# Interleaved rotary embedding, 8 rows: the last output row leaves in one cast DMA of GpSimd's queue, without an fp32 tail on SP's queue

## The chip, the cores and the metric

The kernel runs on one core of one Trainium2 chip. The metric is the device time of one execution in microseconds (us). Before the change it is 316.17 us, the median of three runs (316.14 to 316.25).

## The reference

Input x is float32 with shape (8, 2048, 16, 64): batch, sequence, heads, head dimension. The head dimension holds pairs (x1, x2) side by side, and cos and sin are float32 (2048, 32), one value per sequence position and pair.

```
x1 = x_pairs[..., 0]
x2 = x_pairs[..., 1]
out1 = x1 * cos - x2 * sin
out2 = x1 * sin + x2 * cos
out = stack([out1, out2], axis=-1)      # pairs side by side again, float32
```

It reads 67.1 MB of x and writes 67.1 MB of output.

## The kernel before

**Tiling.** A batch entry is called a row here. The 2048 positions of a row lie on 128 partitions with K = 16 positions each, so a row is a tile of 128 partitions by 16 x 1024 elements. In DRAM it is 8.39 MB of float32, and each partition's part is one contiguous piece of 65,536 bytes. In the on-chip memory it is bf16 and half that size. The pool `buf` (tile name `xt`) has five places for rows; the list `at` says which row uses which place, so that rows 5, 6 and 7 reuse the places of rows 0, 1 and 2 (at = 4, 0, 1, 2, 3, 4, 0, 1).

**Transfers.** `load` (line 57) and `store` (line 60) are DMAs issued by GpSimd (POOL in the profile). They change the type on the way: float32 in DRAM to bf16 on the chip, and back. All of them go through one queue, which the profile calls q0 (software_dynamic). Two transfers go through SP's queue, q1 (hardware_dynamic), which carries them without a change of type: the head (line 94), which is the first four of the sixteen positions of row 0, as fp32 into the tile `st`; and the tail (line 133), which is the last four positions of row 7, as fp32 out of `st`.

**Arithmetic.** VectorE (DVE) does all of it, in bf16. For one row `rotate` issues three instructions: qt = x * s_tab (line 79), x = x * c_tab (line 85), x = x + qt with each pair swapped (line 90). `qt` and `st` share one buffer (tag "work").

**Order.** It is written out by hand (`tc.manual_schedule()`). Loads and stores stand in GpSimd's program in the order of the calls, and GpSimd waits at each one until its data are ready or its place is free. The end of that program, which the change touches, is: store of rows 4 and 5, store of row 6, store of the first 12 positions of row 7. Beside the last of them come three instructions on other engines. VectorE copies a single element from row 7 into row 6's place (line 131); since that place is being read by the store of row 6, VectorE waits there until the store has landed. Then it casts the last four positions of row 7 to fp32 (line 132), and SP sends them (line 133).

**The close.** After the last instruction the framework adds a closing sequence, recorded under line 159. SP waits for the last transfer of each semaphore that DMAs use, two semaphores to a wait, and for VectorE. GpSimd runs a drain of its own. Then the engines meet, GpSimd clears the semaphores, and they meet again.

Of the kernel before, what the change touches and what calls it, by code (L numbers as in the profile page):

```python
# [2 lines left out]

# [4 lines left out]


@with_exitstack  # L10
def kernel(
    ctx: ExitStack,
    tc: tile.TileContext,
    x: bass.AP,
    cos: bass.AP,
    sin: bass.AP,
    out: bass.AP,
):
    nc = tc.nc
    fp32 = mybir.dt.float32  # L20
    bf16 = mybir.dt.bfloat16
    mult = mybir.AluOpType.mult
    add = mybir.AluOpType.add

    B, S, H, D = x.shape
    P = 128
    K = S // P
    D2 = D // 2
    HD = H * D
    NX = 5  # L30
    HEAD = 4
    TAIL = 4
    GATE = 14

    x_t = x.rearrange("b (p k) h d -> p b k (h d)", p=P, k=K)
    out_t = out.rearrange("b (p k) h d -> p b k (h d)", p=P, k=K)
    cos_t = cos.rearrange("(p k) c -> p (k c)", p=P, k=K)
    sin_t = sin.rearrange("(p k) c -> p (k c)", p=P, k=K)

    consts = ctx.enter_context(tc.tile_pool(name="consts", bufs=1))  # L40
    rows_pool = ctx.enter_context(tc.tile_pool(name="rows", bufs=1))
    stage = ctx.enter_context(tc.tile_pool(name="stage", bufs=1))

    cos_sb = consts.tile([P, K * D2], fp32)
    sin_sb = consts.tile([P, K * D2], fp32)
    c_tab = consts.tile([P, K, D], bf16)
    s_tab = consts.tile([P, K, D], bf16)


    buf = rows_pool.tile([P, NX, K, HD], bf16, name="xt")  # L50
    at = [4, 0, 1, 2, 3, 4, 0, 1]

    def place(b, n=1, k0=0, k1=K):
        return buf[:, at[b] : at[b] + n, k0:k1]

    def load(b, n=1, k0=0, k1=K):
        nc.gpsimd.dma_start(out=place(b, n, k0, k1), in_=x_t[:, b : b + n, k0:k1])  # L57

    def store(b, n=1, k0=0, k1=K):
        nc.gpsimd.dma_start(out=out_t[:, b : b + n, k0:k1], in_=place(b, n, k0, k1))  # L60

    def rotate(b, k0=0, k1=K, gate=None):
        nk = k1 - k0
        xp = buf[:, at[b], k0:k1]
        qt = stage.tile([P, K, HD], bf16, name="qt", tag="work")

        def rows(a):
            return a.rearrange("p k (h e) -> p k h e", h=H, e=D)

        def tab(a, j0=0, j1=nk):  # L70
            return dataclasses.replace(
                a,
                offset=a.offset + (k0 + j0) * D,
                ap=[a.ap[0], [D, j1 - j0], [0, H], [1, D]],
            )


        for a, z in ((0, nk),) if gate is None else ((0, GATE), (GATE, nk)):
            nc.vector.tensor_tensor(  # L79
                out=rows(qt[:, a:z]), in0=rows(xp[:, a:z]), in1=tab(s_tab, a, z), op=mult  # L80
            )
            if z < nk:
                one = buf[:1, at[gate], 0, :1]
                nc.vector.tensor_copy(out=one, in_=one)  # L84
        nc.vector.tensor_tensor(out=rows(xp), in0=rows(xp), in1=tab(c_tab), op=mult)  # L85
        q_swap = dataclasses.replace(
            qt, offset=qt.offset + 1, ap=[qt.ap[0], [2, nk * HD // 2], [-1, 2]]
        )
        x3 = xp.rearrange("p k (a j) -> p (k a) j", j=2)
        nc.vector.tensor_tensor(out=x3, in0=x3, in1=q_swap, op=add)  # L90

    with tc.manual_schedule():
        head = stage.tile([P, TAIL, HD], fp32, name="st", tag="work")
        nc.sync.dma_start(out=head[:, :HEAD], in_=x_t[:, 0, :HEAD])
        load(0, k0=HEAD)
        nc.gpsimd.dma_start(out=cos_sb, in_=cos_t)  # L96
        nc.gpsimd.dma_start(out=sin_sb, in_=sin_t)  # L97
        load(1)
        load(2)

        nc.vector.tensor_copy(out=buf[:, at[0], :HEAD], in_=head[:, :HEAD])  # L101
        s2 = s_tab.rearrange("p k (i j) -> p (k i) j", j=2)
        nc.vector.tensor_copy(out=s2[:, :, 0], in_=sin_sb)  # L103
        nc.vector.tensor_scalar_mul(s2[:, :, 1], sin_sb, -1.0)  # L104
        nc.vector.tensor_copy(  # L105
            out=c_tab.rearrange("p k (i j) -> p (k i) j", j=2),
            in_=cos_sb.to_broadcast([P, K * D2, 2]),
        )

        rotate(0, 0, HEAD)  # L110
        rotate(0, HEAD, K)
        rotate(1, gate=0)
        store(0)
        load(3, 2)
        load(5)
        rotate(2)
        store(1, 2)
        rotate(3)
        store(3)
        load(6, 2)  # L120
        rotate(4)
        rotate(5)
        store(4, 2)
        rotate(6)
        store(6)
        rotate(7)
        store(7, k1=K - TAIL)


        tail = stage.tile([P, TAIL, HD], fp32, name="st", tag="work")  # L130
        nc.vector.tensor_copy(out=buf[:1, at[6], 0, :1], in_=buf[:1, at[7], K - 1, :1])  # L131
        nc.vector.tensor_copy(out=tail, in_=buf[:, at[7], K - TAIL :])  # L132
        nc.sync.dma_start(out=out_t[:, 7, K - TAIL :], in_=tail)


# [1 line left out]
_INS = ['x', 'cos', 'sin']  # L137
_OUTS = [((8, 2048, 16, 64), 'float32')]


# [23 lines left out]
```

## Time and profile before

| | |
|---|---|
| median of three runs | 316.17 us |
| the profiled execution | 316.19 us |
| span of its trace (first to last instruction) | 314.4 us |
| time outside the span | 1.8 us |
| DVE busy | 215.1 us (68%) |
| POOL busy | 8.7 us (3%) |
| HBM read, written | 67.63 MB, 67.11 MB |
| DMA packets | 2688 |

The profile is of one execution. Its page gives the busy time of each engine, the span in 40 slices with a digit of busy tenths for each engine and for the 16 DMA engines, the DMA queues, the chain of work that ended last, and the costliest groups of instructions. Bytes are counted at the destination, so a load that writes bf16 counts for half of what it reads. "SPq" and "POOLq" are the instruction sequencers of SP and GpSimd; time in which they wait is not counted as busy. Times that are given to a thousandth are those of single records of this trace, counted from the start of the span.

### The profile page before, as it was taken

What the parts mean: (1) busy time and instruction counts of PE and PEld (TensorE: products, weight loads), DVE (VectorE), ACT (ScalarE), POOL (GpSimd) and SP (SyncE); (2) the same over time, 40 slices, a digit from 0 to 9 for tenths busy, and PEclk for the clock granted to TensorE, in tenths of its full rate; (3) what the DMA queues carried; (4) which work ended last, traced back from release to release, by engine and by line L of the source; (5) the groups of instructions that cost most, each with busy time, mean ns of one, the idle gap of its engine ahead of it and who ended that gap; (6) DMA issues with size and microseconds to landing.
All of it is one profiled execution on the core that took longest, in us unless ns stands there. A gap on an engine that the chain in (4) does not pass through costs nothing.

```text
span 314.4 us, 110 instructions
## 1 busy us (share of the span) xinstructions
DVE 215.1 (68%) x35; POOL 8.7 (3%) x18
## 2 busy tenths in 40 slices
DVE  0029999999999206999999999300009999997200
POOL 3000000100000000000000000000000000000000
DMA  8999999999999999999999999999999999999997
GB/s 261 256 283 200 200 208 258 267 400 425 308 200 200 217 250 200 200 325 475 400 400 500 434 400 400 250 217 200 200 308 425 400 400 525 409 400 400 434 440 327
DMA packets 2688, 102.24 MB, mean 325 GB/s; under 512 B 256, under 2 KB 256, under 8 KB 384
## 3 DMA queue, kind: packets, MB, share of 16 engines
q0 software_dynamic: 2400, 98.04, 96.8%
q1 hardware_dynamic: 288, 4.19, 3.3%
HBM read 67.63 MB, written 67.11 MB: 429 GB/s over the span
## 4 chain that ended last, share of the span: by engine, by line
DVE 59%; another core or an unknown queue 17%; DMA 17%; issue 0%; POOL 0%; DVEq 0%; PEldq 0%
DVE xt L85 19%; DVE xt L90 19%; DVE qt L79 19%; DMA out_dram<-xt 10%; DMA sin_sb<-in_sin_dram 7%; DVE st L132 1%; POOL xt L57 0%; DVE c_tab L105 0%; POOL cos_sb L96 0%; DVE s_tab L103 0%; DVE s_tab L104 0%; DVE xt L131 0%; DVE xt L84 0%; DVEq L79 0%
## 5 line engine op out<-in xcount | busy, mean ns | idle before, releaser
L79 DVE TENSOR_TENSOR qt<-xt,s_tab 128x16384 bf16<-128x16384 bf16 (+4 forms) x10 | 69.8, 6983 | 53.7 <-DMA xt<-in_x_dram 53.5
L90 DVE TENSOR_TENSOR xt<-xt,qt 128x16384 bf16<-128x16384 bf16 (+2 forms) x9 | 69.7, 7744 | 0.3
L85 DVE TENSOR_TENSOR xt<-xt,c_tab 128x16384 bf16<-128x16384 bf16 (+2 forms) x9 | 69.7, 7744 | 0.3
L101 DVE CAST xt<-st 128x4096 bf16<-128x4096 f32 x1 | 2.3, 2294 | 15.3 <-DMA st<-in_x_dram 15.3
L60 POOL DMA_DIRECT2D out_dram<-xt x6 | 3.6, 607 | 227.6 <-DVE xt L90 171.8
L57 POOL DMA_DIRECT2D xt<-in_x_dram x6 | 3.8, 637 | 53.0 <-DMA out_dram<-xt 52.2
L103 DVE CAST s_tab<-sin_sb 128x512 bf16<-128x512 f32 x1 | 0.5, 454 | 6.3 <-DMA sin_sb<-in_sin_dram 6.3
L131 DVE COPY xt<-xt 1x1 bf16<-1x1 bf16 x1 | 0.1, 145 | 5.7 <-DMA out_dram<-xt 5.7
L132 DVE CAST st<-xt 128x4096 f32<-128x4096 bf16 x1 | 2.3, 2272 | 0.0
L105 DVE CAST c_tab<-cos_sb 128x1024 bf16<-128x1024 f32 x1 | 0.7, 682 | 0.0
L97 POOL DMA_DIRECT2D sin_sb<-in_sin_dram x1 | 0.6, 564 | 0.0
L96 POOL DMA_DIRECT2D cos_sb<-in_cos_dram x1 | 0.6, 557 | 0.0
L104 DVE TENSOR_SCALAR s_tab<-sin_sb 128x512 bf16<-128x512 f32 x1 | 0.4, 442 | 0.0
L84 DVE COPY xt<-xt 1x1 bf16<-1x1 bf16 x1 | 0.1, 136 | 0.0
L148 POOL MEMSET const-float32-0.0<- 128x1 f32 x1 | 0.1, 99 | 0.2 <-issue 0.2
L148 POOL MEMSET const-bfloat16-1.0<- 128x1 bf16 x1 | 0.1, 102 | 0.0
L148 POOL MEMSET const-uint8-127<- 128x1 uint8 x1 | 0.1, 100 | 0.0
L148 POOL MEMSET const-float32-1.0<- 128x1 f32 x1 | 0.1, 99 | 0.0
## 6 DMA issues: line engine op xcount, KB each, us to landing
xt<-in_x_dram POOLq DMA_DIRECT2D x2, 8192.0 KB, 58.8
xt<-in_x_dram POOLq DMA_DIRECT2D x3, 4096.0 KB, 57.6
out_dram<-xt POOLq DMA_DIRECT2D x1, 6144.0 KB, 22.2
xt<-in_x_dram POOLq DMA_DIRECT2D x1, 3072.0 KB, 21.3
st<-in_x_dram SPq DMA_DIRECT2D x1, 2048.0 KB, 14.5
out_dram<-st SPq DMA_DIRECT2D x1, 2048.0 KB, 16.9
cos_sb<-in_cos_dram POOLq DMA_DIRECT2D x1, 256.0 KB, 21.3
sin_sb<-in_sin_dram POOLq DMA_DIRECT2D x1, 256.0 KB, 21.4
```

What stands on the lines that cost most here:

```text
L57: nc.gpsimd.dma_start(out=place(b, n, k0, k1), in_=x_t[:, b : b + n, k0:k1])
L60: nc.gpsimd.dma_start(out=out_t[:, b : b + n, k0:k1], in_=place(b, n, k0, k1))
L79: nc.vector.tensor_tensor(out=rows(qt[:, a:z]), in0=rows(xp[:, a:z]), in1=tab(s_tab, a, z), op=mult)
L85: nc.vector.tensor_tensor(out=rows(xp), in0=rows(xp), in1=tab(c_tab), op=mult)
L90: nc.vector.tensor_tensor(out=x3, in0=x3, in1=q_swap, op=add)
L96: nc.gpsimd.dma_start(out=cos_sb, in_=cos_t)
L97: nc.gpsimd.dma_start(out=sin_sb, in_=sin_t)
L101: nc.vector.tensor_copy(out=buf[:, at[0], :HEAD], in_=head[:, :HEAD])
L103: nc.vector.tensor_copy(out=s2[:, :, 0], in_=sin_sb)
L104: nc.vector.tensor_scalar_mul(s2[:, :, 1], sin_sb, -1.0)
L105: nc.vector.tensor_copy(out=c_tab.rearrange("p k (i j) -> p (k i) j", j=2), in_=cos_sb.to_broadcast([P, K * D2, 2]),)
L132: nc.vector.tensor_copy(out=tail, in_=buf[:, at[7], K - TAIL :])
```

## The change

The last row goes out in one call, `store(7)`, of all 16 positions through GpSimd's queue. The tail tile, the one-element copy that waits for the store of row 6, the cast to fp32 and the transfer on SP's queue are removed. The head tile takes its size from HEAD instead of TAIL; both are 4, so nothing changes there. Line numbers behind line 31 are smaller by one, and those behind the removed block by seven.

```
-    TAIL = 4
...
-        head = stage.tile([P, TAIL, HD], fp32, name="st", tag="work")
+        head = stage.tile([P, HEAD, HD], fp32, name="st", tag="work")
...
         rotate(7)
-        store(7, k1=K - TAIL)
-
-
-        tail = stage.tile([P, TAIL, HD], fp32, name="st", tag="work")
-        nc.vector.tensor_copy(out=buf[:1, at[6], 0, :1], in_=buf[:1, at[7], K - 1, :1])
-        nc.vector.tensor_copy(out=tail, in_=buf[:, at[7], K - TAIL :])
-        nc.sync.dma_start(out=out_t[:, 7, K - TAIL :], in_=tail)
+        store(7)
```

In the built programs VectorE has two instructions fewer (the copy and the cast), SP one fewer (the transfer), and GpSimd's last store has 128x16384 elements instead of 128x12288. Everything ahead of it stands in the same order with the same waits. SP's five closing waits come in another pairing, since the semaphore of its second transfer is gone. Before they are, in order: {store 7, store 6}, then three pairs of older transfers, then {tail, an older load}. After they are: {store 6}, {store 7, an older one}, then three pairs of older transfers.

## Prediction

> **What bounds the kernel.** I read the page first (engines, slices, queues), then the windows of the end, the timeline of the end, the waits of SP's queue, and the records of the closing line. From the page:
>
> ```profile
> DVE 215.1 (68%) x35; POOL 8.7 (3%) x18
> ...
> DMA  8999999999999999999999999999999999999997
> ...
> q0 software_dynamic: 2400, 98.04, 96.8%
> q1 hardware_dynamic: 288, 4.19, 3.3%
> ```
>
> No compute engine is above 68%, while the DMA digit is 9 from the second slice to the last but one, and the two queues together fill 96.8 + 3.3 = 100% of the 16 DMA engines' time. The transfers are the bound from start to end. The chain of waits names mostly DVE, but it also has 17% of "another core or an unknown queue", and DVE's own waits end on a load; DVE follows the transfers.
>
> The end of the kernel, from the timeline (start, duration, what; in brackets the idle time before it):
>
> ```profile
> 262.75 0.55 POOL L60 DMA_DIRECT2D out_dram<-xt  x1 [62.80 <-DVE xt L90]
> ...
> 279.94 8.69 DVE L90 TENSOR_TENSOR xt<-xt,qt 128x16384 bf16<-128x16384 bf16 x1
> 288.92 0.55 POOL L60 DMA_DIRECT2D out_dram<-xt  x1 [25.63 <-DVE xt L90]
> 294.28 0.14 DVE L131 COPY xt<-xt 1x1 bf16<-1x1 bf16 x1 [5.65 <-DMA out_dram<-xt]
> 294.35 2.27 DVE L132 CAST st<-xt 128x4096 f32<-128x4096 bf16 x1
> 296.65 0.35 SPq L133 DMA_DIRECT2D out_dram<-st  x1
> ```
>
> Row 7 is computed at 288.63, and its store is issued at 288.92. The store of row 6, issued at 262.75, lands only at 294.19, where L131 is released. So store 7 stands in its queue for some 4 us before the first of its packets runs. The windows show how full the DMA engines are in the two last rows (columns: stretch, length, DVE and POOL busy, clock, DMA share, GB/s):
>
> ```profile
> 274.01:293.32 19.31, 14.59 (x2) 0.55 (x1) 1.00 1.02 434
> 293.32:312.69 19.37, 2.34 (x2) 0.00 (x0) 1.00 1.02 433
> ```
>
> The first stretch is the packets of store 6, all on q0: 8.39 MB at 434 GB/s. The second is row 7, three quarters on q0 and one quarter on q1: the same bytes at 433 GB/s. There is no hole that the change could fill, and the split over two queues brings no rate.
>
> **Part 1: the transfer of row 7.** Before, a DMA engine serves 8 packets of 49,152 bytes on q0 and 32 of 16,384 bytes on q1. After, it serves 8 of 65,536 bytes on q0, as for row 6. In the packet records the 65,536-byte packets of store 6 follow each other every 2.412 us on an engine, and from the completion record of one row to that of the next (stores 5 and 6) it is 293.803 - 274.487 = 19.316 us on the engine that ends last. The mixed stretch takes 2.430 us for 49,152 + 16,384 bytes, and the 16,384-byte packets alone, with which it ends, one every 0.607 us (2.428 us for 65,536 bytes). So the last completion record moves from 313.233 to 293.803 + 19.316 = 313.119: **-0.11 us**. Bounds: 0 (both rates equal) and -0.15 (8 x 0.018). Nothing else delays store 7: its one wait is DVE L90 of row 7, as before, and its packets queue behind those of row 6, as before (between stores 5 and 6 the engine goes on 0.042 us after the completion record).
>
> A rule of the Trainium skill speaks against the change (DMA: Bandwidth & Descriptors, Specifications): a transfer of GpSimd's queue has its first byte after about 1 us, one of SP's after about 0.6 us. By it alone the last bytes would come some 0.4 us later, an estimate from that page. In this trace that start is covered: the store is issued over 4 us before its first packet at 293.336 can run.
>
> **Part 2: what is removed on DVE and SP.** L131 (0.14), L132 (2.27) and the issue of L133 (0.35) lie beside the packets of q0, which run from 293.336 to 310.799 without a hole. Nothing else waits for them but L133 itself. Their removal is worth nothing; DVE is done at 288.63, over 24 us ahead of the end. The extra 4,096 elements a partition cost GpSimd's issue nothing: the whole-row store took 0.55 us too (262.75).
>
> **Part 3: the close.** This is where the change shifts something. SP's waits and the closing records:
>
> ```profile
> SPq L159 <- DMA out_dram<-xt: 14.1, 1, 14.1
> SPq L159 <- DMA out_dram<-st: 2.2, 1, 2.2
> ```
>
> ```profile
> L159 SPq EVENT_SEMAPHORE  x7: 17/28/28, 311.2 to 314.4; - x7
> ...
> L159 POOLq DRAIN  x3: 45/96/22855, 288.9 to 314.1; - x3
> ```
>
> Before, q0 is done first. Its last completion record is at 310.799, and SP passes the wait for it at 311.156 (0.357 later). SP then passes three older waits (0.074 + 0.061 + 0.060 = 0.195 us) while the tail still runs, waits 2.2 us more, and passes the tail's wait at 313.580. GpSimd's first drain is the long one in the second fence: it starts at 288.902 and takes 22.855 us, so it ends at 311.757, which is 0.958 us after q0's last completion record. The tail on q1 covers that end: the engines meet only at 313.736, 0.156 us after SP's last wait, two short drains of SP lying between (0.065 and 0.058, then 0.033).
>
> After, q0 is the last, and both covers are gone.
> - SP: 313.119 + 0.357 = 313.476 for the wait of store 7, then the three older waits in the open (0.195), then 0.156: 313.827, **+0.09 us** against 313.736.
> - GpSimd's drain: 313.119 + 0.958 = 314.077, and 0.03 to its next instruction (the distance after its second drain): 314.106, **+0.37 us**.
>
> The later one counts. No other record shows what the long drain waits for. Bounds: if its end follows nothing of q0, it is out of the way and SP's +0.09 is left; if its delay grows with the size of the store behind it, 0.958 x 65,536 / 49,152 = 1.277 us and the sum is +0.69. I take the delay of the one row there is, 0.958.
>
> **Sum.** The profiled execution took 316.19 us (0.02 above the median). 316.19 + 0.37 = **316.56 us**; the -0.11 of the transfer is inside the 0.37. About 0.2% (0.63 us) is what a measurement of this kernel can tell from no change, so I forecast no change that counts, on the slow side of zero.
>
> **The rivals.**
> 1. *SP's chain ends last* (GpSimd's drain ends for a reason of its own): 316.19 + 0.09 = 316.28. For it: the drain's record has no wait for a semaphore, and POOL spans are rough. Against it: the drain ended within 1 us of q0's last packet after standing for 22.9 us. 19 in 100.
> 2. *Slower: GpSimd's drain trails longer.* The place is the close, where the tail gave it 313.736 - 311.757 = 2.0 us of cover; without cover it decides over 0.2% once its delay after the last completion record exceeds 0.958 + 0.26 = 1.22 us. By bytes it would be 1.277 us: 316.19 + 0.69 = 316.88. For it: a single row, and bigger packets. Against it: the same number of packets on q0 (128 and 16 completion records). 14 in 100.
> 3. *Slower: q0 starts afresh for row 7* instead of going on. On the empty queue at the start, from the issue at 1.24 to the first packet at 5.397 it took 4.2 us: 316.56 + 4.2 = 320.8 at most. Against it: stores 5 and 6 went on within 0.042 us with the same size. 4 in 100. The Trainium skill's 0.4 us for such a start (the page and section of part 1), again an estimate, would make it 316.96; no row here shows that price.
> 4. *The close costs nothing more*, and only the transfer's -0.11 is left: 316.08. It needs SP's older waits to pass for free, and they took 0.195 us. 5 in 100.
> 5. *Faster by over 0.2%*: it would need a loss on the shared engines that the packet records don't show; they leave 0.15 at most. 4 in 100.
>
> That the change does not do what it says is out: the built program has neither cast nor SP transfer, and a whole last store.
>
> **Chances and range.** The forecast has 54 in 100. Within 0.2%: forecast, rival 1 and rival 4, 54 + 19 + 5 = 78. Slower: 14 + 4 = 18. Faster: 4. The range goes from rival 4 to rival 2, 316.05 to 316.90, and leaves out rivals 3 and 5.
>
> **What would show it.** In the changed profile: no L131 to L133; the packets of row 7 at 434 GB/s without a hole behind those of row 6, with q0's last completion record near 313.1; SP's wait for the last store near 313.5 and three short waits behind it; the long drain of GpSimd ending near 314.1 and the span near 314.8. A span near 314.5 with the drain ending early is rival 1. A drain that ends over 1.2 us behind the last packet is rival 2. A hole between the two last rows is rival 3. The forecast is wrong if the rate of the last row differs from 434 GB/s, or if anything moves ahead of 288.92.

## The result, and the profile after

The changed kernel takes 316.59 us (median of 22 runs, 316.51 to 316.80); the kernel before took 316.17 us in 22 runs beside them (316.04 to 316.33). The ratio is 1.0014, with a 95% interval of 1.0008 to 1.0019. The change makes the kernel slower by 0.42 us: less than 0.2%, clear of zero, and close to the forecast of 316.56. The profiled execution took 316.77 us with a span of 315.0 us.

From the page of the changed kernel, first the engines, the DMA digits and the queues:

```profile
DVE 212.8 (68%) x33; POOL 8.6 (3%) x18
...
DMA  8999999999999999999999999999999999999996
...
q0 software_dynamic: 2400, 100.14, 98.1%
q1 hardware_dynamic: 144, 2.10, 1.8%
```

VectorE has lost 2.3 us of work and q1 its 2.1 MB of tail. The DMA engines are as full as before. The last digit falls from 7 to 6: the end of the kernel holds more time without packets. The windows of the two last rows (stretch, length, DVE and POOL busy, clock, DMA share, GB/s):

```profile
274.01:293.32 19.31, 14.77 (x2) 0.54 (x1) 1.00 1.02 434
293.32:312.69 19.37, 0.00 (x0) 0.00 (x0) 1.00 1.01 433
```

Row 7 runs at the rate of row 6 here too, so neither kernel has time to win in the transfer. The timeline of the end is now one line, the issue of the whole last store:

```profile
280.12 8.69 DVE L89 TENSOR_TENSOR xt<-xt,qt 128x16384 bf16<-128x16384 bf16 x1
289.10 0.54 POOL L59 DMA_DIRECT2D out_dram<-xt  x1 [25.63 <-DVE xt L89]
```

What changed is behind the packets. The records of the closing line (durations shortest/median/longest in ns, starts of the first and last):

```profile
L152 SPq EVENT_SEMAPHORE  x7: 17/28/28, 294.4 to 314.9; - x7
L152 POOLq DRAIN  x3: 45/81/25206, 289.1 to 314.7; - x3
```

GpSimd's long drain starts at 289.082 and lasts 25.206 us, to 314.288. The next table follows the end of both profiled executions through single records:

| record, us from the start of the span | before | after |
|---|---|---|
| last completion of store 6 (q0) | 293.803 | 293.972 |
| last completion on q0 | 310.799 | 313.288 |
| last completion on q1 | 313.233 | at the start only |
| SP passes its last wait for an output | 313.580 | 313.686 |
| GpSimd's long drain ends | 311.757 | 314.288 |
| SP's last drain before the engines meet begins | 313.703 | 313.992 |
| GpSimd's next record, where they meet | 313.736 | 314.332 |

Before, the engines meet 0.033 us after SP's drain begins, and GpSimd's has been over for 2.0 us. After, SP's drain begins at 313.992 and the meeting comes 0.044 us after the end of GpSimd's drain: SP stands ready for 0.3 us.

To take out that store 6 itself ended 0.17 us later in this execution, count from its last completion. Before, the meeting is 313.736 - 293.803 = 19.933 us behind it, after it is 314.332 - 293.972 = 20.360: +0.43 us. Two terms make it up. The transfer of row 7 went from 19.430 to 19.316, which is -0.11; the close, from the last completion to the meeting, went from 0.503 to 1.044, which is +0.54.

### The profile page after: what moved, and what is told of

It reads as the page before. It is cut to its first block, busy times and chain, and to the rows that moved or that the text cites. A ratio compares the mean times of both kernels' runs of the same rounds, so it can differ in the third digit from the quotient of the medians.

```text
span 315.0 us, 106 instructions
## 1 busy us (share of the span) xinstructions
DVE 212.8 (68%) x33; POOL 8.6 (3%) x18
## 4 chain that ended last, share of the span: by engine, by line
DVE 59%; another core or an unknown queue 17%; issue 9%; DMA 7%; POOL 1%; POOLq 0%; DVEq 0%; PEldq 0%
DVE xt L84 19%; DVE xt L89 19%; DVE qt L78 19%; DMA sin_sb<-in_sin_dram 7%; POOL xt L56 0%; DVE c_tab L104 0%; POOLq L152 0%; POOL out_dram L59 0%; POOL cos_sb L95 0%; DVE s_tab L102 0%; DVE s_tab L103 0%; DVE xt L83 0%; DVEq L78 0%; PEldq L152 0%
```

## The experiments

The theory: the time is lost because q0 is last, so that GpSimd's drain, which ends about 1 us behind q0's last completion, comes out from behind the tail on q1. Rivals: the amount sent over q1 counts; the cast on the way, or the size of the store, costs; VectorE's removed work plays a part. All seven kernels write the whole output. Each was compared with the kernel before on the same chip, whose median was 316.18 us for the first four and 316.16 for the last three.

### One position of row 7 over SP's queue, and one position of row 6

First, the kernel before with a shorter tail:

```
-    TAIL = 4
+    TAIL = 1
...
-        head = stage.tile([P, TAIL, HD], fp32, name="st", tag="work")
+        head = stage.tile([P, HEAD, HD], fp32, name="st", tag="work")
```

> The kernel before with a tail of one position of row 7 in place of four (0.5 MB on SP's queue in place of 2.1 MB). My theory: what the tail gave is an end on SP's queue that comes after GpSimd's queue is done, so that GpSimd's drain (about 1.0 us after the last completion on its queue) ends out of sight. Eight small packets an engine should still leave some four of them behind the last packet of GpSimd's queue, about 0.5 us; the drain and SP's chain then end within some 0.1 us of each other: 316.1 to 316.3 us. Rival: what counts is how much of the row goes over SP's queue; a quarter of the tail keeps a quarter of the 0.42 us: about 316.5.

Second, the changed kernel with the same amount on SP's queue, but earlier:

```
         rotate(6)
-        store(6)
+        store(6, k1=K - 1)
+        tail = stage.tile([P, 1, HD], fp32, name="st6", tag="tail")
+        nc.vector.tensor_copy(out=tail, in_=buf[:, at[6], K - 1 :])
+        nc.sync.dma_start(out=out_t[:, 6, K - 1 :], in_=tail)
         rotate(7)
         store(7)
```

> The changed kernel, but one position of row 6 (not of row 7) is cast to fp32 and goes over SP's queue; row 7 leaves whole on GpSimd's queue. The same bytes on each queue as with the one-position tail of row 7, only that SP's transfer ends well before the end. My theory: GpSimd's queue is last, its drain ends last, about 1.0 us after the last completion: 316.5 to 316.7 us, like the changed kernel. Rival: it is the use of both queues that pays, or the cast on the way that costs: then the same time as with the one-position tail of row 7, 316.1 to 316.5.

The tail of row 7 took 316.30 us (ratio 1.0000, interval 0.9992 to 1.0009), the tail of row 6 316.70 (1.0015, 1.0006 to 1.0024). Both queues carry the same bytes in both kernels, and the last completion of all comes at the same time in the two profiles (313.159 and 313.158). What differs at the end is which queue it is on, and the medians are 0.40 us apart. In the waits of SP's queue, the first kernel has a last wait for q1's transfer:

```profile
SPq L159 <- DMA out_dram<-xt: 17.7, 1, 17.7
...
SPq L159 <- DMA out_dram<-st: 0.2, 1, 0.2
```

The second has none: its transfer on q1 was long over.

```profile
SPq L155 <- DMA out_dram<-xt: 50.1, 1, 50.1
```

GpSimd's long drain stands in the closing records of the two kernels as the longest of three (in ns):

```profile
L159 POOLq DRAIN  x3: 45/88/24859, 288.8 to 314.1; - x3
```

```profile
L155 POOLq DRAIN  x3: 45/96/24751, 289.4 to 314.6; - x3
```

With the tail of row 7, q1's last completion comes 0.472 us behind q0's (313.159 and 312.687), and GpSimd's drain ends at 313.693, beside SP's last drain at 313.644; the engines meet at 313.737. This is the edge at which the drain comes out of cover. In the kernel with row 6, q0 is last at 313.158 and the drain ends at 314.178, while SP's last drain begins at 313.956; the engines meet at 314.222. The rival on the amount, which gave about 316.5 for the first kernel, falls.

### The last store in two, all on GpSimd's queue

```
-        store(7)
+        store(7, k1=K - 4)
+        store(7, k0=K - 4)
```

> The changed kernel with the last row's store cut in two on GpSimd's queue: 12 positions, then 4. My theory: the drain trails the last completion by the same 1.0 us, and nothing else moves but some 0.05 us for the extra completion and the smaller packets: 316.55 to 316.75 us. Rival: the drain's delay grows with the size of the store behind it; a quarter of the size gives about 0.25 us, SP's chain ends last, and the time is 316.2 to 316.35.

It took 316.67 us (1.0014, 1.0005 to 1.0023). The last store's packets are 16,384 bytes in place of 65,536, and the drain still ends 1.072 us after the last completion (313.063 and 314.135). The delay does not shrink with the size, so the price by bytes of the prediction's rival 2 falls.

### VectorE's two instructions put back into the changed kernel

```
         store(7)
+
+        tail = stage.tile([P, 4, HD], fp32, name="st", tag="work")
+        nc.vector.tensor_copy(out=buf[:1, at[6], 0, :1], in_=buf[:1, at[7], K - 1, :1])
+        nc.vector.tensor_copy(out=tail, in_=buf[:, at[7], K - 4 :])
```

> The changed kernel with VectorE's two removed instructions put back: the one-element copy that waits for the store of row 6, and the fp32 cast of the last four positions, whose result is sent nowhere. My theory: they ran beside the packets of the last row and their removal was worth nothing: 316.55 to 316.75 us, the time of the changed kernel. Rival: part of the change's cost or gain comes from VectorE's end (its drain, its share of the on-chip memory): then the time moves by 0.2 us or more, either way.

It took 316.58 us (1.0011, 1.0002 to 1.0020), the changed kernel 316.59. The copy and the cast cost nothing, since they stand beside 19 us of packets.

### Tails of two, four and eight positions

```
-    TAIL = 4
+    TAIL = 2
...
-        head = stage.tile([P, TAIL, HD], fp32, name="st", tag="work")
+        head = stage.tile([P, HEAD, HD], fp32, name="st", tag="work")
```

> The kernel before with a tail of two positions in place of four. My theory: only the distance between the end of GpSimd's queue and the end of SP's queue counts. With two positions it is about 1.2 us, more than the 0.5 us at which the drain comes out of cover, so the time is that of the kernel before within 0.15 us: 316.05 to 316.3. Rival (the amount sent over SP's queue counts): half of the 0.42 us is lost, about 316.4.

It took 316.12 us (0.9998, 0.9989 to 1.0007): all of the cover is kept with half of the tail. q1 ends 0.923 us behind q0 (313.073 and 312.150; the expectation said about 1.2), the drain at 313.146, and SP's chain is last at 313.564.

The next kernel has eight positions and no one-element copy:

```
-    TAIL = 4
+    TAIL = 8
...
-        head = stage.tile([P, TAIL, HD], fp32, name="st", tag="work")
+        head = stage.tile([P, HEAD, HD], fp32, name="st", tag="work")
...
-        nc.vector.tensor_copy(out=buf[:1, at[6], 0, :1], in_=buf[:1, at[7], K - 1, :1])
```

> The kernel before with a tail of eight positions of row 7, and without the one-element copy that makes the cast wait for the store of row 6. GpSimd's queue carries half of row 7 and ends several us before SP's. My theory: the drain ends about 1.0 us after the last completion on GpSimd's queue, so some us before the end, and the time is that of the kernel before within 0.15 us, 316.0 to 316.3. Rival: the drain doesn't follow GpSimd's queue but ends near the end of the program: then it ends near 313 to 314 us as in the changed kernel, and the time is about 316.5. If SP's queue were slower than GpSimd's by more than the packets show (0.5%), 0.2 us or more would come on top.

It took 316.32 us (1.0003, 0.9994 to 1.0011), 0.02 us above the expected range. The drain ends at 311.939, 1.026 us after q0's last completion at 310.913 and 1.9 us before the engines meet at 313.865. A drain that follows the end of the program would have ended near the end; it follows q0. Here the timeline shows something that was not expected, of which more below:

```profile
288.65 4.43 DVE L131 CAST st<-xt 128x8192 f32<-128x8192 bf16 x1
288.92 4.28 POOL L60 DMA_DIRECT2D out_dram<-xt  x1 [25.63 <-DVE xt L90]
293.11 0.35 SPq L132 DMA_DIRECT2D out_dram<-st  x1
```

Last, the kernel before (four positions) without the one-element copy alone:

```
-        nc.vector.tensor_copy(out=buf[:1, at[6], 0, :1], in_=buf[:1, at[7], K - 1, :1])
```

> The kernel before without the one-element copy, so that the cast of the tail runs right behind row 7 and SP's transfer is issued near 291 us in place of 296.7. In the run with eight positions GpSimd's issue of the last store stood still for 4.28 us, until 0.12 us after the cast beside it ended. My theory: the same happens here for the 2.3 us of the shorter cast, the store is issued by 291.1, over 2 us before its packets can run, and costs nothing. SP's packets begin some 3 packets of the other queue after their issue, near 297 to 298, and still end about 1 us behind GpSimd's queue, so the drain stays covered: 316.05 to 316.3 us. Rival: SP's packets pair up with the other queue's from the start, GpSimd's queue is last, and the drain comes out of cover: 316.5 to 316.7.

It took 316.18 us (0.9995, 0.9987 to 1.0004). SP's transfer is issued at 290.952 in place of 296.653, its packets begin at 297.021 in place of 302.760, and q1 ends 0.613 us behind q0 (313.232 and 312.619; the expectation said about 1 us). The drain ends at 313.593, SP's last drain begins at 313.714: still covered, by 0.12 us, in place of 1.95. The copy buys a margin and no time.

### The drain in all nine traces

| kernel | last completion on q0 | drain ends | delay, us | median, us |
|---|---|---|---|---|
| before | 310.799 | 311.757 | 0.958 | 316.17 |
| tail of eight, no wait | 310.913 | 311.939 | 1.026 | 316.32 |
| tail of two | 312.150 | 313.146 | 0.996 | 316.12 |
| tail of four, no wait | 312.619 | 313.593 | 0.974 | 316.18 |
| tail of one, row 7 | 312.687 | 313.693 | 1.006 | 316.30 |
| last store in two | 313.063 | 314.135 | 1.072 | 316.67 |
| tail of one, row 6 | 313.158 | 314.178 | 1.020 | 316.70 |
| VectorE's work kept | 313.181 | 314.198 | 1.017 | 316.58 |
| after | 313.288 | 314.288 | 1.000 | 316.59 |

The delay stays within 0.96 to 1.07 us, with last packets of 16,384 to 65,536 bytes and with q0's end moving over 2.5 us. The four kernels in which q0 is last take 316.58 to 316.70, the five in which q1 is last 316.12 to 316.32.

The semaphore events of the traces are sharper than the completion records. At the end of a store its semaphore gets sixteen updates, and SP's wait for the last store passes 0.016 to 0.017 us behind the last of them. GpSimd's drain ends 0.618 or 0.619 us behind the last update for its last store in eight of the nine traces, and 0.659 in the kernel with two stores. The spread of the table lies mostly ahead of the update: from the completion record to the update it takes 0.340 to 0.413 us.

That the drain ends by q0 is shown by how it moves; what it does in the 0.62 us inside GpSimd no record names, and that was not tried.

## Why the prediction was right

**The transfer (-0.11).** Right: 19.430 to 19.316 us, counted from store 6. One count in the working is a slip: a DMA engine serves 8 packets of 16,384 bytes on q1, not 32 (2.1 MB over 128 packets and 16 engines). No term of the sum used it.

**VectorE's and SP's removed work (0).** Right: with VectorE's two instructions put back the time is the same within 0.01 us. The rule of the Trainium skill about first bytes (DMA: Bandwidth & Descriptors, Specifications) had no room to act, as argued: in the changed trace the last completions of stores 6 and 7 are 19.316 us apart, the distance of stores 5 and 6 before.

**The close.** The step that carries the result, and right in its mechanism. SP's older waits came into the open, but SP's last drain began at 313.992, and GpSimd's drain ended 0.296 us later. The size was a little low: from the last completion to the meeting it is 1.000 + 0.044 in place of 0.958 + 0.03, which is the 0.056 us between +0.371 forecast and +0.427 in the profiles. The medians say +0.42. The 0.958 was a single row, and that a single row was enough is luck: the nine of the table spread over only 0.11 us.

**What can be told.** The prediction put at 0.63 us what a measurement can tell from no change, and so forecast a change that does not count. With 22 runs of each kernel the interval of the ratio, 1.0008 to 1.0019, leaves out 1, so the 0.42 us were told from zero.

**The rivals.** SP's chain as the last (316.28), and a close that costs nothing (316.08), fall with SP standing ready for 0.3 us. The longer drain (316.88) falls with its 1.000 us behind 65,536-byte packets, where the price by bytes was 1.277, and with the row of the store in two. A fresh start of q0 (320.8) falls with the distance of 19.316 us. Nothing made the kernel faster.

## What to carry to other kernels

Here the bytes fill the DMA engines up to the end, and splitting them over two queues brought no rate, but which queue ended last counted: look at what each engine still does after its own last transfer. A small transfer on SP's queue that ended 0.6 us or more behind GpSimd's hid a drain of 1 us, 0.47 us was the edge, and two positions did it as well as four. Removing work beside a full queue saved nothing, and what that work covered had to be priced by itself.

## What was not expected of the hardware

**GpSimd's DMA issue stood still beside the cast.** With the fp32 cast running, the issue of the last store took 4.28 us (it ends at 293.199, the cast at 293.082) and 2.15 us (291.045, the cast at 290.925), in place of 0.55: each time until 0.12 us after the cast's end. Beside a bf16 tensor-tensor instruction of VectorE the issue takes 0.55 (262.75 in the kernel before, beside L79), as it does alone (288.92). The Trainium skill describes such a stop (SBUF — State Buffer, SBUF: two separate sides: GpSimd cannot write descriptors while VectorE holds the port pair that they share, until about 115 ns after the VectorE instruction). The two rows agree with it. With four positions and no wait the issue ends 2.3 us before the first DMA engine is free (store 6's first completion is at 293.381) and costs nothing: row 7's first packets begin 0.04 us behind the completions of store 6, as in all the other kernels but one. With eight positions it ends 0.3 us before (293.504), and that was too late: the first packets begin 0.24 us behind the completions on average (0.15 to 0.27). This hole is large enough for the 0.14 us by which this kernel is above the kernel before; no run takes it out alone.

**A transfer on SP's queue starts late behind a full GpSimd queue.** From issue to first packet it took 1.00 us on empty engines (the head, 0.743 to 1.746). It took 6.11 (before), 6.32, 7.52 and 6.07 us (tails of two, of one, of four without the wait) and 6.13 (the position of row 6) while q0's packets ran, each of them 1.8 to 2.4 us long, and 4.27 with the tail of eight, where they are 1.2 us long. So it fits a wait by q0's packets better than a fixed time: in most of these traces about three of them begin on an engine in that time (2.1 to 3.8 in all six, counted over the 16 engines up to the first packet of q1). Why so many was not tried.
